# Reordering the input phase of a two-layer diffusion step: inputs first, squares folded on VectorE, seven accumulators, the condition store moved behind the last activation

## The chip, the cores and the metric

The program runs on one core of a Trainium2 chip, as one launch. The metric is the device time of one execution in microseconds. The engines of the core are named as in the profile: PE (TensorE matmul), PEld (its weight loads), DVE (VectorE), ACT (ScalarE), POOL (GpSimd) and SP (SyncE, which here only issues DMAs). A suffix q, as in SPq or ACTq, marks an instruction of an engine's own queue, here always the issue of a DMA.

## The reference

One inference step through two layers over 128 context tokens and 256 latent tokens, 384 in all, of width 2048. Layer 0 mixes RWKV-7 heads and a Fourier mixer, layer 1 is windowed attention. What the change touches is the entry of layer 0:

```python
sh_p, sc_p, g_p = _modulation(c_ctx, mod_w[layer], mod_b[layer])   # silu(cond) @ w + b, split in three
sh_s, sc_s, g_s = _modulation(c, mod_w[layer], mod_b[layer])
hp = _rmsnorm(xp, norm_pre[layer]) * (1.0 + sc_p) + sh_p
hs = _rmsnorm(xs, norm_pre[layer]) * (1.0 + sc_s) + sh_s
...
proj = h @ w_in          # r, k, v, the low-rank inputs, gates and the Fourier inputs
```

So the first projection needs the mean of the squares of each token, and a shift and a scale that come out of a product of the two conditions with a 2048 x 6144 matrix of 4-byte numbers, of which layer 0 needs 2/3 at its entry (32 loads of 1 MB).

## The kernel before

All matrices are held with the channel on the partition (128) and the 384 tokens along the row. A projection is done as three matmuls for each 128x128 block of weights (high and low part of the weights and of the activations: `hhi`, `hlo`, `whi`, `wlo`), 128x384 each.

**The stream of weights.** `Stream` issues 256 KB loads `raw<-we` on SP's queue into two buffers. ACT casts a loaded unit to `whi` (line 260), DVE subtracts to get `wlo` (line 261), and three such pairs may be held. A unit feeds 12 projection matmuls. `plan` puts the units into the order in which the input phase uses them.

**The input phase** is `layer0_in`. It loads the modulation weights in 32 loads `mraw<-modw` of 1 MB into seven buffers, also on SP's queue; `mod_unit` multiplies each with the conditions (`ps_mod<-mraw,silu`). After each four of them ACT copies the sums out (`mrow`, line 331), PE turns them into columns (`ps_mt`), and DVE adds the bias (line 338). Four loads give the shift of a block of four channel tiles, the next four its scale; there are four such blocks, b = 0 to 3. The inputs `xT` come in four loads of 768 KB behind the first four modulation loads. ACT squares each of the 16 channel tiles (`sq`, line 649), and PE adds them up over the partitions with a matrix of ones (`ps_ss`). After the reciprocal root, `make_h` makes the normalised activations of a block: two ACT instructions a tile, then a cast and a subtraction on DVE. Each block of activations is then fed at once to the accumulators that are open: `low` (256 wide, two units a block) and r, k, v of head pair 0 and r of head pair 1, six units a block, 24 in all. A generator list `first` names them, and `pieces` hands out one unit a step:

```python
        ahead = rkv(0, (None, self.pw, self.pw)) + rkv(1, (self.pw, None, None))
        first = [(self.proj_cm(256, acts, low_done), 2)] + [(g, 1) for g in ahead[:4]]
```

`None` means a bank of the PSUM pool `pa` (three banks), `self.pw` one of `pw` (five banks), which `ps_mod` and `ps_mt` use as well.

**What sets the order.** A scheduler orders the instructions of each engine when the program is built, by priority and by its own idea of durations; the queue of each engine then runs in that order. Each DMA of SP and ACT signals one of eight counters, DMAHW0 to DMAHW7, which are given out in turn over both queues. A DMA that takes a counter again waits until the DMA that had it before has landed.

**The condition store.** `build` writes the 2 x 2048 conditions to DRAM (`sd<-cth`, line 604, on ACT's queue), where they are read back much later (`srow<-sd`, line 812). The store is 16 KB in runs of four numbers (16 bytes), 1024 runs.

**After the input phase** the projections go on, interleaved with the RWKV work (`wkv_elem`, `wkv_lower`, `wkv_solve`, `wkv_chain`) and with the remaining modulation columns, whose weights come in 512 KB loads `rawf<-modw` (line 795) into one buffer; each feeds four PE groups `ps_mod<-rawf,silu`, and the next load may be issued when they are done.

Of the kernel before, what the change touches and what calls it, by code (L numbers as in the profile page):

```python
# [11 lines left out]
F32 = mybir.dt.float32  # L12
# [8 lines left out]
KT = 16  # L21
# [284 lines left out]
class K:  # L306
# [69 lines left out]
    def plan(self):  # L376

        A = self.A
        w = [("w", A[n][i]) for n in ("we", "weo", "wo", "woo") for i in range(A[n].shape[0])]
        n0 = A["we"].shape[0]  # L380
        n1 = n0 + A["weo"].shape[0]
        for n in (n1, len(w)):
            w[n - 4:n] = [x + (i,) for i, x in enumerate(w[n - 4:n])]

        w[:24] = [w[i] for b in range(4) for i in (2 * b, 2 * b + 1, 8 + b, 12 + b, 16 + b, 20 + b)]
        out, at = [], 0
        for a, b, jobs in ((n0 - 56, n1 - 10, DVE_MODS[0]), (n1 + 48, len(w) - 68, DVE_MODS[1])):
            m = self.mod_items(jobs)
            if jobs is DVE_MODS[0]:

                q = self.mod_items(PE_MODS)
                m = [x for i in range(12) for x in m[i:i + 1] + q[8 * i // 12:8 * (i + 1) // 12]]
            m = list(chain.from_iterable(m))
            out += w[at:a]
            for i in range(b - a):
                out += m[len(m) * i // (b - a):len(m) * (i + 1) // (b - a)]
                out.append(w[a + i])
            at = b
        return out + w[at:]
# [120 lines left out]
    def make_h(self, pool, kt, src, sc, sh):  # L520
# [4 lines left out]
        for cnd, sl in ((1, slice(0, TP)), (0, slice(TP, T))):  # L525
            nc.scalar.activation(h[:, sl], src[:, sl], AF.Identity, bias=sh[:, m, cnd:cnd + 1],
                                 scale=sc[:, m, cnd:cnd + 1])
        hi = self.hp.tile([128, T], F32R, name="hhi", tag="hhi", bufs=KT)
# [30 lines left out]
    def build(self):  # L559
# [4 lines left out]
        with ExitStack() as ctx:  # L564
# [36 lines left out]
            self.sd = self.dp.tile([4, 2, 128, 4], F32, name="sd")  # L601
            sq = th.rearrange("p (q c k) -> p q c k", q=4, c=2)
            nc.vector.tensor_copy(sq, self.silu[:, 0:32].rearrange("p (q k c) -> p q c k", q=4, c=2))
            nc.scalar.dma_start(self.sd.rearrange("q c p k -> p q c k"), sq)
            self.macc = {}
# [8 lines left out]
    def layer0_in(self, acts, first):  # L614
# [20 lines left out]

        for _ in range(4):
            load()
        xT = ip.tile([128, KT, T], F32, name="xT")
        for b in range(4):
            nc.sync.dma_start(xT[:, 4 * b:4 * b + 4], A["xT"][:, 4 * b:4 * b + 4])  # L640
        for _ in range(3):
            load()
        mod(4)
        ones = ip.tile([128, 128], F32, name="ones")
        nc.vector.memset(ones, 1.0)
        ps = self.pa.tile([128, 512], F32, name="ps_ss", tag="acc")
        for kt in range(KT):
            sq = ip.tile([128, T], F32, name="sq", tag="sq", bufs=2)
            nc.scalar.activation(sq, xT[:, kt], AF.Square)
            self.mm(ps[:, :T], ones, sq, start=(kt == 0), stop=(kt == KT - 1))  # L650
        rs = ip.tile([128, T], F32, name="rs")
# [6 lines left out]
        for b in range(4):  # L658
# [7 lines left out]
            for i in range(7):  # L666
                mod(1)
                if i >= 1:
                    next(pieces[i - 1])
        self.close("mp")  # L670
# [3 lines left out]
    def layer0_mix(self):  # L674
# [20 lines left out]

        ahead = rkv(0, (None, self.pw, self.pw)) + rkv(1, (self.pw, None, None))
        first = [(self.proj_cm(256, acts, low_done), 2)] + [(g, 1) for g in ahead[:4]]
        self.layer0_in(acts, first)
# [24 lines left out]
        def proj_lane():  # L723
# [4 lines left out]
            for j in range(1, 8):  # L728

                gens = ahead[4:] if j == 1 else rkv(j)  # L730
                for g in gens:
# [855 lines left out]
```

## Time and profile before

| what | us |
|---|---|
| median of 3 runs | 1600.47 |
| lowest and highest run | 1600.28 and 1605.43 |
| profiled execution, its own time | 1596.4 |
| its span (first to last instruction) | 1594.6 |

The profiled execution lies 4.1 us below the median of the three runs. The span leaves out 1.8 us that lie around it. Times in the views are counted from the start of the span.

### The profile page before, as it was taken

The numbers are of one execution on the slowest core, as the hardware profiler recorded it, in microseconds if no ns is written. First come the engines' busy times: TensorE is split into PE (matmuls) and PEld (weight loads), VectorE is DVE, ScalarE is ACT, GpSimd is POOL, SyncE is SP. The second block draws the span as 40 slices with busy tenths as digits, with TensorE's granted clock in tenths as the row PEclk, the third lists the DMA queues.
The fourth block names the chain that finished last, engine by engine and source line by source line (L and its number), as shares of the span: only waits on it lengthen the run. The fifth ranks groups of instructions, "written<-read, shape, count | busy, mean of one in ns | idle before, by whom it ended". The sixth has DMA issues, their size and how long they took to land.

```text
span 1594.6 us, 30005 instructions
## 1 busy us (share of the span) xinstructions
PE 1507.3 (95%) x11488; PEld 1275.6 (80%) x11488; DVE 1069.1 (67%) x2584; ACT 810.9 (51%) x1771; POOL 3.9 (0%) x21
## 2 busy tenths in 40 slices
PE   7789999989998999999999998999999999999997
PEld 2557778767776778879998778988888889998777
DVE  1426896687777685574665755899878999653344
ACT  3326756857656655454333335744556555343332
POOL 0000000000000000000000000000000000000000
PEclk9899999999999999999999999899999999999999
DMA  9985352354333243444558664565322444447443
GB/s 365 375 311 164 123 160 78 102 167 122 97 107 110 86 143 90 132 152 126 174 189 325 211 207 144 200 225 204 100 73 73 133 132 140 125 122 242 125 120 139
DMA packets 120246, 255.74 MB, mean 160 GB/s; under 512 B 12324, under 2 KB 45220, under 8 KB 109732
## 3 DMA queue, kind: packets, MB, share of 16 engines
q1 hardware_dynamic: 111528, 235.97, 44.8%
q10 hardware_dynamic: 8576, 17.86, 3.2%
q8 instruction: 90, 1.47, 0.4%
q14 instruction: 52, 0.43, 0.1%
HBM read 246.40 MB, written 7.39 MB: 159 GB/s over the span
## 4 chain that ended last, share of the span: by engine, by line
PE 64%; DVE 16%; DMA 11%; ACT 6%; issue 3%; ACTq 0%; DVEq 0%; SPq 0%
PE acc L404 31%; PE acct L404 16%; DMA rawf<-modw 5%; DVE wlo L261 3%; PE ps_mod L406 3%; DVE junk L350 2%; DMA raw<-we 2%; DMA mraw<-modw 1%; DMA raw<-modw 1%; PE ps_o L410 1%; PE ps_v L410 1%; PE ps_pv L410 1%; ACT whi L260 1%; PE ps_s L410 1%; PE ps_sa L410 1%
## 5 line engine op out<-in xcount | busy, mean ns | idle before, releaser
L260 ACT CAST whi<-raw 128x512 fp32r<-128x512 f32 x480 | 295.5, 621 | 444.7 <-PE acc L404 196.5
L261 DVE TENSOR_TENSOR wlo<-raw,whi 128x512 fp32r<-128x512 f32 x480 | 327.5, 688 | 275.6 <-ACT whi L260 270.8
L404 PE MATMUL acc<-hhi,whi 128*128 128x384 f32 x1376 | 478.3, 348 | 12.5 <-ACT whi L260 5.7
L404 PE MATMUL acc<-hlo,whi 128*128 128x384 f32 x1376 | 472.9, 344 | 0.0
L404 PE MATMUL acc<-hhi,wlo 128*128 128x384 f32 x1376 | 470.7, 343 | 1.7 <-DVE wlo L261 1.3
L404 PEld LDWEIGHTS acc<-hhi,whi 128*128 128x128 f32 x1376 | 261.3, 190 | 44.2 <-issue 18.1
L404 PEld LDWEIGHTS acc<-hlo,whi 128*128 128x128 f32 x1376 | 261.3, 190 | 13.7 <-issue 11.9
L404 PEld LDWEIGHTS acc<-hhi,wlo 128*128 128x128 f32 x1376 | 260.9, 190 | 11.1 <-issue 5.5
L350 DVE SCALAR_TENSOR_TENSOR junk<-raw,srow 128x512 f32<-128x512 f32 x224 | 154.1, 688 | 8.6 <-DMA raw<-modw 5.2
L404 PE MATMUL acct<-whi,yhi 128*128 128x512 f32 (+1 forms) x432 | 154.4, 358 | 2.4 <-DVE yb L1318 2.1
L404 PE MATMUL acct<-wlo,yhi 128*128 128x512 f32 (+1 forms) x432 | 153.9, 356 | 0.0
L404 PE MATMUL acct<-whi,ylo 128*128 128x512 f32 (+1 forms) x432 | 153.7, 356 | 0.0
L404 PEld LDWEIGHTS acct<-whi,yhi 128*128 128x128 f32 x432 | 81.5, 189 | 20.7 <-DVE yb L1318 6.5
L404 PEld LDWEIGHTS acct<-whi,ylo 128*128 128x128 f32 x432 | 81.5, 189 | 12.4 <-issue 0.2
L404 PEld LDWEIGHTS acct<-wlo,yhi 128*128 128x128 f32 x432 | 81.5, 189 | 11.8
L406 PE MATMUL ps_mod<-rawf,silu 128*32 128x256 f32 x112 | 35.0, 395 | 22.5 <-DMA rawf<-modw 22.3
L406 PE MATMUL ps_mod<-mraw,silu 128*32 128x512 f32 x64 | 35.5, 668 | 9.7 <-DMA mraw<-modw 9.7
L1118 DVE TENSOR_TENSOR work<-work 128x30 f32<-128x30 f32 (+14 forms) x120 | 39.2, 327 | 2.1
L1120 DVE TENSOR_TENSOR work<-work 128x30 f32<-128x30 f32 (+14 forms) x120 | 39.2, 327 | 1.9
L1538 DVE TENSOR_REDUCE ast<-ps_sa 128x1 f32<-128x384 f32 x64 | 25.3, 415 | 20.3 <-PE ps_sa L410 20.1
L406 PEld LDWEIGHTS ps_mod<-rawf,silu 128*32 128x32 f32 x112 | 7.7, 108 | 36.2 <-DMA rawf<-modw 25.6
L410 PE MATMUL ps_mod<-rawf,silu 128*32 128x256 f32 x336 | 35.9, 395 | 0.0
(331 smaller groups left out, 2286.5 us busy)
## 6 DMA issues: line engine op xcount, KB each, us to landing
raw<-we SPq DMA_DIRECT2D x200, 256.0 KB, 2.9
raw<-wo SPq DMA_DIRECT2D x160, 256.0 KB, 2.7
raw<-modw SPq DMA_DIRECT2D x36, 1024.0 KB, 5.2
mraw<-modw SPq DMA_DIRECT2D x32, 1024.0 KB, 8.9
rawf<-modw SPq DMA_DIRECT2D x56, 512.0 KB, 3.9
raw<-weo SPq DMA_DIRECT2D x64, 256.0 KB, 2.9
raw<-woo SPq DMA_DIRECT2D x64, 256.0 KB, 2.7
G<-gd ACTq DMA_DIRECT2D x4, 1024.0 KB, 7.4
```

Of the source, the lines that this page charges most:

```text
L260: k.nc.scalar.copy(hi, raw)
L261: k.nc.vector.tensor_tensor(lo, raw, hi, op=ALU.subtract)
L350: nc.vector.scalar_tensor_tensor(junk, raw[:, 512 * i:512 * i + 512], 1.0, self.srow[:, c], op0=ALU.mult, op1=ALU.mult, accum_out=self.dac ...
L404: op(*args, **kw)
L406: self.head.append(op(*args, **kw).ins)
L410: op(*args, **kw)
L1118: TT(tv, X[:, s + 1:32, s:s + 1].to_broadcast([128, n, s]), X[:, s:s + 1, 0:s].to_broadcast([128, n, s]), op=ALU.mult)
L1120: TT(X[:, s + 1:32, 0:s], X[:, s + 1:32, 0:s], tv, op=ALU.add)
L1538: nc.vector.tensor_reduce(st[:, 0, i:i + 1], src[i], axis=AX.X, op=ALU.max)
```

## The change

In `layer0_in` the four loads of the inputs go to the head of SP's queue, behind two units of weights, and the first seven modulation loads follow in one go. The squares are taken by ACT in four instructions of four tiles each; DVE adds the four tiles to one in two instructions; PE does one `ps_ss` matmul for each four tiles, four instead of 16, and the first four modulation units stand behind it instead of ahead of it. Seven accumulators (k of head pair 1 is added, in `pw`) take a unit in each block instead of six, so 28 units belong to the input phase. The condition store is made after the last `make_h`: its ACT issue is tied behind the last activation.

```diff
-        w[:24] = [w[i] for b in range(4) for i in (2 * b, 2 * b + 1, 8 + b, 12 + b, 16 + b, 20 + b)]
+        w[:28] = [w[i] for b in range(4) for i in (2 * b, 2 * b + 1, 8 + b, 12 + b, 16 + b, 20 + b, 24 + b)]
...
-            sq = th.rearrange("p (q c k) -> p q c k", q=4, c=2)
-            nc.vector.tensor_copy(sq, self.silu[:, 0:32].rearrange("p (q k c) -> p q c k", q=4, c=2))
-            nc.scalar.dma_start(self.sd.rearrange("q c p k -> p q c k"), sq)
+            self.th = th
...
-        for _ in range(4):
-            load()
         xT = ip.tile([128, KT, T], F32, name="xT")
         for b in range(4):
             nc.sync.dma_start(xT[:, 4 * b:4 * b + 4], A["xT"][:, 4 * b:4 * b + 4])
-        for _ in range(3):
+        for _ in range(7):
             load()
-        mod(4)
         ones = ip.tile([128, 128], F32, name="ones")
         nc.vector.memset(ones, 1.0)
+
         ps = self.pa.tile([128, 512], F32, name="ps_ss", tag="acc")
-        for kt in range(KT):
-            sq = ip.tile([128, T], F32, name="sq", tag="sq", bufs=2)
-            nc.scalar.activation(sq, xT[:, kt], AF.Square)
-            self.mm(ps[:, :T], ones, sq, start=(kt == 0), stop=(kt == KT - 1))
+        for b in range(4):
+            sq = ip.tile([128, 4, T], F32, name="sq", tag="sq", bufs=2)
+            nc.scalar.activation(sq, xT[:, 4 * b:4 * b + 4], AF.Square)
+            nc.vector.tensor_tensor(sq[:, 0:2], sq[:, 0:2], sq[:, 2:4], op=ALU.add)
+            nc.vector.tensor_tensor(sq[:, 0], sq[:, 0], sq[:, 1], op=ALU.add)
+            self.mm(ps[:, :T], ones, sq[:, 0], start=(b == 0), stop=(b == 3))
+        mod(4)
...
             for i in range(7):
                 mod(1)
-                if i >= 1:
-                    next(pieces[i - 1])
+                next(pieces[i])
+
+        sq = self.th.rearrange("p (q c k) -> p q c k", q=4, c=2)
+        nc.vector.tensor_copy(sq, self.silu[:, 0:32].rearrange("p (q k c) -> p q c k", q=4, c=2))
+        with self.tc.issue_after(self.last_h.ins):
+            nc.scalar.dma_start(self.sd.rearrange("q c p k -> p q c k"), sq)
...
-        ahead = rkv(0, (None, self.pw, self.pw)) + rkv(1, (self.pw, None, None))
-        first = [(self.proj_cm(256, acts, low_done), 2)] + [(g, 1) for g in ahead[:4]]
+        ahead = rkv(0, (None, self.pw, self.pw)) + rkv(1, (self.pw, self.pw, None))
+        first = [(self.proj_cm(256, acts, low_done), 2)] + [(g, 1) for g in ahead[:5]]
...
-                gens = ahead[4:] if j == 1 else rkv(j)
+                gens = ahead[5:] if j == 1 else rkv(j)
```

Where the scheduler then puts things is seen at three places. The first is the head of SP's queue, its first rows (`raw` is a unit of projection weights, `mraw` a modulation load). Before:

```order
L236 DMA raw<-we 128x512 x2
L628 DMA mraw<-modw 128x2048 x4
L640 DMA xT<-xT 128x1536 x4
L628 DMA mraw<-modw 128x2048 x14
L236 DMA raw<-we 128x512 x2
L628 DMA mraw<-modw 128x2048
```

With the change:

```order
L236 DMA raw<-we 128x512 x2
L636 DMA xT<-xT 128x1536 x4
L626 DMA mraw<-modw 128x2048 x17
L236 DMA raw<-we 128x512 x2
L626 DMA mraw<-modw 128x2048
```

The inputs stand ahead of all modulation loads, and 17 of these instead of 18 stand ahead of the third and fourth unit of weights.

The second place is ACT's queue where block b = 2 gets its activations (`h_688` and so on are the four tiles of the block, `sh`, `sc` its shift and scale). Before:

```order
L331 COPY mrow<-ps_mod 128x512
L526 ACTIVATE h_688<-xT,sh_107,sc_108 128x128
L526 ACTIVATE h_688<-xT,sh_107,sc_108 128x256
L526 ACTIVATE h_695<-xT,sh_107,sc_108 128x128
L526 ACTIVATE h_695<-xT,sh_107,sc_108 128x256
L526 ACTIVATE h_702<-xT,sh_107,sc_108 128x128
L526 ACTIVATE h_702<-xT,sh_107,sc_108 128x256
L526 ACTIVATE h_709<-xT,sh_107,sc_108 128x128
L526 ACTIVATE h_709<-xT,sh_107,sc_108 128x256
L260 CAST whi<-raw 128x512 x3
```

With the change:

```order
L526 ACTIVATE h_695<-xT,sh_105,sc_106 128x128
L526 ACTIVATE h_695<-xT,sh_105,sc_106 128x256
L526 ACTIVATE h_702<-xT,sh_105,sc_106 128x128
L526 ACTIVATE h_702<-xT,sh_105,sc_106 128x256
L260 CAST whi<-raw 128x512
L526 ACTIVATE h_709<-xT,sh_105,sc_106 128x128
L526 ACTIVATE h_709<-xT,sh_105,sc_106 128x256
L526 ACTIVATE h_716<-xT,sh_105,sc_106 128x128
L526 ACTIVATE h_716<-xT,sh_105,sc_106 128x256
L260 CAST whi<-raw 128x512 x3
```

One cast of a unit of weights now stands between the second and the third tile of the block instead of behind the fourth.

The third place is SP's queue at the end of the input phase, with the counters that each issue waits for. With the change the store `sd` takes counter DMAHW7 on ACT's queue, right behind the last activation, and SP has these rows (`rawf` is a later modulation load):

```order
L236 DMA raw_850<-we 128x512 [waits DMAHW5_49,DVE_49]
L798 DMA rawf_1084<-modw 128x4x256 [waits PE_49]
L236 DMA raw_880<-we 128x512 [waits DMAHW6_49,DVE_49]
L236 DMA raw_928<-we 128x512 [waits DMAHW7_49,DMAHW0_49,DVE_49]
L798 DMA rawf_1102<-modw 128x4x256 [waits DMAHW2_49,PE_49]
```

Before, the store had counter DMAHW0 and stood near the start, and the sixth modulation load (`mraw_129`) took that counter next:

```order
L640 DMA xT_122<-xT 128x1536 [waits DMAHW6_49]
L628 DMA mraw_127<-modw 128x2048 [waits DMAHW7_49]
L628 DMA mraw_129<-modw 128x2048 [waits DMAHW0_49]
L628 DMA mraw_131<-modw 128x2048 [waits DMAHW1_49]
L628 DMA mraw_138<-modw 128x2048 [waits DMAHW2_49,PE_49]
```

The load that has to wait for the store to land was a modulation load near the start; now it is `raw_928`, a unit of weights (the 26th of 28), with the second `rawf` load queued behind it.

## Rows read from the trace of the kernel before

**Rows 1.** The page: span, and part 1 for PE.
```profile
span 1594.6 us, 30005 instructions
PE 1507.3 (95%) x11488; PEld 1275.6 (80%) x11488; DVE 1069.1 (67%) x2584; ACT 810.9 (51%) x1771; POOL 3.9 (0%) x21
```

**Rows 2.** Windows: busy us of each engine, granted clock, DMA share, GB/s.
```profile
24.00:28.00 4.00, 4.00 (x11) 1.77 (x9) 0.00 (x0) 2.24 (x5) 0.00 (x0) 1.00 0.47 144
28.00:62.00 34.00, 25.68 (x154) 12.28 (x152) 13.25 (x16) 11.38 (x21) 0.00 (x0) 0.90 1.02 421
100.00:124.00 24.00, 23.77 (x137) 16.01 (x138) 4.15 (x9) 4.69 (x8) 0.46 (x4) 0.93 0.67 252
...
200.00:250.00 50.00, 47.08 (x459) 38.97 (x460) 47.69 (x128) 32.06 (x59) 0.13 (x1) 1.00 0.46 143
```

**Rows 3.** Timeline of SP's issues, 11 to 30 us: start, duration.
```profile
11.18 0.43 SPq L628 DMA_DIRECT2D mraw<-modw  x1
25.80 3.03 SPq L628 DMA_DIRECT2D mraw<-modw  x6
```

**Rows 4.** Waits of SP's queue, 0 to 30 us: total, times, longest.
```profile
SPq L628 <- DMA sd<-cth: 14.2, 1, 14.2
```

**Rows 5.** DMA issues, 0 to 30 us: KB each, median us to landing.
```profile
sd<-cth ACTq DMA_DIRECT2D x1, 16.0 KB, 18.6
```

**Rows 6.** Packets of ACT's DMA queue, 11 to 14 us and 25 to 25.2 us.
```profile
q10 hardware_dynamic: 166, 0.00, 3.1%
...
q10 hardware_dynamic: 58, 0.00, 16.3%
```

**Rows 7.** Timeline of PE, 60 to 124 us: start, duration, idle before and releaser.
```profile
63.33 0.69 PE L404 MATMUL acc<-hhi,whi 128*128 128x384 f32 x1 [2.51 <-ACT whi L260]
...
98.99 0.44 PE L404 MATMUL acc<-hhi,whi 128*128 128x384 f32 x1 [3.08 <-ACT whi L260]
...
100.07 0.44 PE L404 MATMUL acc<-hhi,wlo 128*128 128x384 f32 x1 [0.46 <-DVE wlo L261]
...
123.07 0.81 PE L410 MATMUL ps_mt<-sel,mrow 128*128 128x2 f32 x6
```

**Rows 8.** Timeline of DVE and ACT, 94 to 130 us.
```profile
94.10 0.17 DVE L338 TENSOR_TENSOR sc<-ps_mt,modb 128x8 f32<-128x8 f32 x1 [9.16 <-PE ps_mt L410]
...
94.50 1.86 ACT L526 ACTIVATE h<-xT,sh,sc 128x128 f32<-128x128 f32 x4 [1.55 <-DVE sc L517]
...
98.33 1.12 ACT L260 CAST whi<-raw 128x512 fp32r<-128x512 f32 x2
...
129.07 0.35 ACTq L899 DMA_DIRECT2D scan<-cscan  x1
```

**Rows 9.** Groups by line, 0 to 46 us: busy, mean ns, idle before.
```profile
L404 PE MATMUL ps_ss<-sq,ones 128*128 128x384 f32 x32 | 14.6, 607 | 0.0
...
L649 ACT ACTIVATE sq<-xT 128x384 f32<-128x384 f32 x16 | 8.3, 522 | 7.3 <-PE ps_ss L404 6.7
L661 DVE TENSOR_TENSOR xT<-xT,rs 128x1536 f32<-128x1536 f32 x4 | 6.8, 1752 | 0.0
...
L653 DVE RECIPROCAL rs<-rs 128x384 f32<-128x384 f32 x1 | 2.6, 2552 | 15.3 <-ACT rs L652 15.3
```

**Rows 10.** The windows view for the modulation matmuls alone (tile mraw).
```profile
63.30:124.00 60.70, 16.86 (x128) 2.98 (x128) 0.94 0.77 293
```

**Rows 11.** Waits of PE, 120 to 150 us.
```profile
PE ps_mod L406 <- DMA rawf<-modw: 3.1, 2, 1.9
```

**Rows 12.** The chain that ended last, 120 to 150 us: start, duration.
```profile
136.54 4.80 DMA rawf<-modw
...
142.03 4.54 PE acc L404 x25
```

**Rows 13.** The page, part 6: KB each, median us from issue to landing.
```profile
raw<-we SPq DMA_DIRECT2D x200, 256.0 KB, 2.9
```

**Rows 14.** Waits of PE, 130 to 700 us.
```profile
PE ps_mod L406 <- DMA rawf<-modw: 22.3, 20, 4.8
```

More of the change, by code (lines that the diff above doesn't have):

```diff
@@ L525, in make_h @@
         for cnd, sl in ((1, slice(0, TP)), (0, slice(TP, T))):
-            nc.scalar.activation(h[:, sl], src[:, sl], AF.Identity, bias=sh[:, m, cnd:cnd + 1],
-                                 scale=sc[:, m, cnd:cnd + 1])
+            self.last_h = nc.scalar.activation(h[:, sl], src[:, sl], AF.Identity, bias=sh[:, m, cnd:cnd + 1],
+                                               scale=sc[:, m, cnd:cnd + 1])
         hi = self.hp.tile([128, T], F32R, name="hhi", tag="hhi", bufs=KT)
```

## The prediction

> **What bounds the kernel now.** The page comes first: PE is busy for 1507 of 1594.6 us [rows 1], so the stages after the entry are short of PE time, and what can be won lies where PE stands idle, which the page puts into its first slices. The windows view then splits the entry. From 28 to 62 us the DMA engines move 421 GB/s with a share of 1.02 [rows 2]: the modulation loads set the pace there, and PE waits. From 24 to 28 us the share is only 0.47 [rows 2], in the middle of a stage that waits for loads. SP's timeline says why: a modulation load is issued at 11.18, the next one at 25.80 [rows 3], and the waits of SP's queue name the condition store as releaser, 14.2 us [rows 4]. The store took 18.6 us to land [rows 5], although it is 16 KB: from 11 to 14 us, beside the large loads, ACT's queue got 166 packets through, which is 166 / 16 engines in 3 us, or 0.29 us each; from 25 to 25.2 us, with the large packets gone, it got 58 through, or 0.055 us each [rows 6].
>
> The second thing that bounds the entry is PE itself, from 63.33 on: there it waited 2.51 us for the third unit of weights [rows 7], which stands behind 18 modulation loads, and then it works nearly without a gap, but for one at 96 to 100 us. There the scale of block 2 was written at 94.10, ACT made eight activations from 94.50, and only at 98.33 came to the casts of weights that PE needed [rows 8]; PE stood for 3.08 us, and 0.46 more for `wlo` [rows 7].
>
> **The change, part by part.** The sum is made on the profiled execution, 1596.4 us, and carried to the median, 1600.47, by subtraction.
>
> *Squares.* ACT takes four tiles in one instruction; that costs at most 4 x 0.522 = 2.1 us [rows 9]. The DVE adds are 768 and 384 wide, each less than the 1.75 us of the 1536-wide product [rows 9]. PE has four `ps_ss` matmuls, 8 rows of 0.61 instead of 32 (14.6 us) [rows 9]. The four inputs are 3.1 MB, 7.5 us at 421 GB/s, and are in at about 13 us. Behind the last of them stand at most 2.1 + 3.5 + 1.2 + 2 (root and its table) + 2.6 (reciprocal) + 7.0 (products), which is 31.4. The scale of block 0 needs eight modulation loads behind the inputs: 13 + 8 x 2.5 = 33. So all of it is hidden, and I put it at 0; if it were late by some us, only the 24 matmuls on the two units loaded at the start would move, and these end well before 58 us. The 11 us of PE time saved by fewer `ps_ss` is worth nothing for the same reason: loads set the pace there.
>
> *a. The wait for the store* leaves the start. The DMA engines then don't run dry: 4 us x (1 - 0.47) = 2.1 us [rows 2].
>
> *b. One modulation load fewer* stands ahead of the third unit: 1.049 MB at 421 GB/s is 2.5 us. The Trainium skill (DMA: Bandwidth & Descriptors, section Bandwidth) says that loads from HBM are bound by about 358 GB/s a core; by that this term would be an estimated 2.9 us and the sum 0.4 us more. The row shows 421 over 34 us, and the row decides. With a and b PE gets its third unit at 63.33 - 4.6 = 58.7.
>
> *c. The gap at block 2.* One cast now stands behind four activations instead of eight: 94.50 + 1.86 = 96.4 instead of 98.33 [rows 8], 1.9 us. One modulation unit of PE, 16.86 / 16 = 1.05 us [rows 10], moves out of the gap and has to be done elsewhere. Net 0.9.
>
> *d. The clock.* From 100 to 124 us, behind the gap, the granted clock was 0.93 [rows 2], which cost 24 x 0.07 = 1.7 us. A shorter gap may keep it. Between 0 and 1.7 I take half, 0.8.
>
> *e. PSUM.* Four of the five `pw` banks are now held by accumulators, so a modulation group can't start before DVE has read the columns of the group before it. Where a modulation unit stands right behind `ps_mt` on PE (two places), that costs the DVE instruction, 0.17 us [rows 8], and the handovers, together 0.3 each: -0.6. Elsewhere projections stand between. Bounds: 0, and twice as much.
>
> a to e give 5.7 us. The four units of k that move into the phase change nothing in this: they are 48 matmuls of 4.54 / 25 = 0.18 us [rows 12] that PE has to do in any case.
>
> *f. The end of the phase.* The last `ps_mt` ended at 123.07 + 0.81 = 123.88 [rows 7]; now 24 more projection matmuls stand ahead of it (4.4 us), so it ends at 123.88 - 5.7 + 4.4 = 122.6. The last activation comes 5.2 us later (`scan` was issued right behind it at 129.07, [rows 8]); there the store is issued: 127.8. When does it land? 64 packets for each engine at 0.055 us are 3.5 us; the fixed part I take from a 256 KB load, 2.9 us less the 0.6 of its bytes at 421 GB/s [rows 13], 2.3. That is 5.8, if nothing else moves. The loads of weights beside it are some 16 packets of 2 KB and 32 of 1 KB an engine, 2.5 us at 26 GB/s an engine: 8.3. The other end is the 18.6 of [rows 5], beside 8 KB packets. The row for free packets is nearer; I take 7.0, the middle of 5.8 and 8.3.
>
> Until then SP stands at `raw_928`, and behind it the second `rawf` load. So that is issued at 127.8 + 7.0 + 0.4 = 135.2 and lands 4.8 us later [rows 12], at 140.0. PE comes to it after 79 matmuls and one group: 122.6 + 14.4 + 0.5 = 137.5, and waits 2.5 us. Without the store it would wait for its buffer only, to 138.6. Before, the two such waits there were 3.1 us [rows 11]; the first now vanishes, since its load stands ahead of fewer units. So f is +0.6, with 1.8 at a store of 5.8 us and -0.7 at 8.3.
>
> Sum: 2.1 + 2.5 + 0.9 + 0.8 - 0.6 + 0.6 = 6.3 us. That gives 1590.1 for an execution like the profiled one, and 1594.2 against the median. What a measurement here can tell from no change is about 0.3%, 4.8 us, so this is not far beyond it.
>
> **The rivals.**
>
> *The store blocks SP (slower).* If beside the weight loads it takes the 18.6 us of before, SP is free at 146.4, the `rawf` load lands at 151.6, PE waits 14.1 us instead of 3.1, and a to f become -5.3: 1605.8. It breaks even where the landing takes 13.3 us. For it speaks that the only landing on record is 18.6; against it that the packets beside it then were four to eight times as large. Chance 0.12.
>
> *The gain is absorbed.* In the RWKV stage DVE is busy 47.69 of 50 us (200 to 250) [rows 2]. Its first chain starts with k of head pair 0, which comes behind the second `rawf` wait and so no earlier than before. If DVE and that chain set the pace, PE only gains slack, and the time stays at 1599 to 1602. Against it: PE is 95% busy [rows 1], and head pair 1, which the first solve needs as well, has its k 48 matmuls earlier. Chance 0.28. With it goes a PSUM wait of more than a microsecond at each of the six modulation groups (e at ten times its price): 1600, chance 0.03.
>
> *More than that.* PE waits 22.3 us for `rawf` loads at 20 places between 130 and 700 us [rows 14]. The new order shifts all of them; if a third goes, 7 us more are won: 1587. Chance 0.13. A shift that loses as much is in the case above.
>
> **How the numbers follow.** My forecast has 0.44, of which 0.02 ends within 0.3%. Faster by over 0.3%: 0.42 + 0.13 = 0.55. Within: 0.28 + 0.03 + 0.02 = 0.33. Slower: 0.12. The predicted time is 1594.2. The range goes from 1586 (the third rival, a little further) to 1602 (the end of the second); what is left out is most of the first rival and the tails. The likeliest case alone, with c to f at their bounds, is 1591 to 1597.
>
> **What would show it.** After the change SP's waits near the start no longer name `sd`, and the windows from 24 to 28 us have a DMA share near 1 (a). The first `acc` matmul that waits for a cast comes near 58.7 (a, b). At block 2 PE waits less than 2 us for `whi` (c), and the granted clock behind it is nearer 1 (d). PE's waits name DVE `sh` or `sc` for under 1 us in all (e). SP waits for `sd` near 130 us, by 1 to 4 us, and PE's second `rawf` group waits 1 to 4 us (f). The prediction is wrong if that wait is over 10 us, or if the entry ends 6 us earlier by PE's count of matmuls and the lead is gone at 300 us.

## The result and the profile after

The change made the kernel slower: 1608.09 us (median of 14 runs, 1604.53 to 1620.46) against 1601.48 us for the kernel before (14 runs, 1596.69 to 1607.46) on the same chip. The ratio is 1.0052, with a 95% interval of 1.0034 to 1.0070. A second measurement on another chip (run e7_after_again below) gave 1607.36 against 1602.55 and 1.0034 (1.0014 to 1.0053). The forecast was 1594.2 us, a gain.

The profiled execution of the changed kernel took 1616.38 us, above its median; that of before, 1596.4, was below its own. So no difference of these two traces alone is taken for an effect. Each kernel was profiled once more, in e7_after_again (1604.38 us) and e8_before_again (1604.36 us).

The page of the changed kernel, its span and its engines, beside [rows 1]:

```profile
span 1614.5 us, 29927 instructions
PE 1519.3 (94%) x11464; PEld 1284.9 (80%) x11464; DVE 1076.0 (67%) x2592; ACT 808.2 (50%) x1759; POOL 3.9 (0%) x21
```

PE is busy for 12 us more, though 24 matmuls went. A busy PE at the lower clock takes longer: the result lists a mean granted clock of 0.972 for this execution and 0.984 for that of before.

**The input phase went as forecast.** Windows of the changed kernel, as [rows 2], and the timeline of SP's issues, as [rows 3]:

```profile
24.00:28.00 4.00, 2.53 (x24) 1.13 (x16) 4.00 (x4) 0.59 (x1) 0.00 (x0) 1.00 1.02 422
28.00:62.00 34.00, 25.38 (x139) 13.68 (x140) 6.81 (x15) 7.24 (x14) 0.00 (x0) 0.77 0.97 394
100.00:124.00 24.00, 23.84 (x149) 15.88 (x142) 3.75 (x9) 4.59 (x8) 0.74 (x4) 0.98 0.68 258
```

```profile
1.66 3.56 SPq L636 DMA_DIRECT2D xT<-xT  x4
5.26 39.97 SPq L626 DMA_DIRECT2D mraw<-modw  x17
45.28 0.90 SPq L236 DMA_DIRECT2D raw<-we  x2
```

The DMA share between 24 and 28 us rose from 0.47 to 1.02. Seventeen loads now follow the inputs without a hole. The granted clock from 28 to 62 us is 0.77 instead of 0.90, but in the second traces of both kernels it is 0.85, so this is not taken for an effect. Timeline of PE in the changed kernel, as [rows 7]: the first `acc` matmul that waits for a cast, the one behind the scale of block 2, and the last `ps_mt`:

```profile
58.25 0.69 PE L404 MATMUL acc<-hhi,whi 128*128 128x384 f32 x1 [2.76 <-ACT whi L260]
...
94.69 0.69 PE L404 MATMUL acc<-hhi,whi 128*128 128x384 f32 x1 [1.54 <-ACT whi L260]
...
122.82 0.81 PE L410 MATMUL ps_mt<-sel,mrow 128*128 128x2 f32 x6
```

The third unit of weights comes at 58.25 instead of 63.33; the gap at block 2 is 1.54 us instead of 3.08 and 0.46. The waits of PE for columns, 56 to 124 us, and for `rawf` loads, 120 to 150 us (as [rows 11]), and the store's landing (as [rows 5]):

```profile
PE ps_mod L406 <- DVE sc L338: 0.3, 1, 0.3
PE ps_mod L406 <- DVE sh L338: 0.3, 1, 0.3
```

```profile
PE ps_mod L406 <- DMA rawf<-modw: 0.2, 1, 0.2
```

```profile
sd<-cth ACTq DMA_DIRECT2D x1, 16.0 KB, 3.5
```

**The lead is gone at the first solve.** Counted along ACT's timeline, the 29th cast of weights stands at 152.69 in the kernel before and at 146.72 in the changed one. That is a lead of 6.0 us. Fifty us later it is a lag. Timeline of DVE and ACT, first solve (`work<-DB`) and start of the first chain (`work<-v`); first the kernel before in its second trace, then the changed kernel:

```profile
197.54 1.91 DVE L1112 STREAM_TRANSPOSE work<-DB 128x1024 f32<-128x1024 f32 x1 [0.71 <-ACT DB L1063]
249.21 1.10 ACT L1175 COPY work<-v 128x256 f32<-128x256 f32 x4
```

```profile
203.06 1.95 DVE L1115 STREAM_TRANSPOSE work<-DB 128x1024 f32<-128x1024 f32 x1
255.49 1.12 ACT L1178 COPY work<-v 128x256 f32<-128x256 f32 x4
```

The second trace of the changed kernel has 201.16 and 253.57, the first of before 198.24 and 249.28. So the first solve comes 3 to 6 us later, and the first chain 4 to 6.

The chain itself makes this up: the second solve starts at the same time again. Timeline of DVE, the kernel before in its second trace, then the changed kernel (the other two traces have 326.27 and 324.67):

```profile
326.20 2.00 DVE L1112 STREAM_TRANSPOSE work<-DB 128x1024 f32<-128x1024 f32 x1
```

```profile
326.48 1.96 DVE L1115 STREAM_TRANSPOSE work<-DB 128x1024 f32<-128x1024 f32 x1
```

What is missing by then is projection work on PE, which is counted below, under theory F.

Why the first solve is late is seen in ACT's queue. Timeline of ACT, the kernel before in its second trace (`kk`, `sq`, `p`, `tha` belong to head pair 0, `work` to pair 1):

```profile
145.54 0.61 ACT L955 ACTIVATE kk<-k,par 128x384 f32<-128x384 f32 x1
...
149.87 0.53 ACT L961 ACTIVATE sq<-sq 128x384 f32<-128x384 f32 x1
...
155.19 0.57 ACT L910 ACTIVATE k<-acc,imu 128x384 f32<-128x384 f32 x1
...
156.24 1.36 ACT L977 ACTIVATE p<-ps_lo,wa 128x256 f32<-128x256 f32 x4 [0.22 <-PE ps_lo L404]
...
157.98 0.87 ACT L980 ACTIVATE p<-p 128x768 f32<-128x768 f32 x1
```

And the changed kernel:

```profile
147.25 0.61 ACT L958 ACTIVATE kk<-k,par 128x384 f32<-128x384 f32 x1
...
152.32 0.62 ACT L958 ACTIVATE work<-k,par 128x384 f32<-128x384 f32 x1 [1.08 <-DVE k L916]
152.96 1.28 ACT L964 ACT_TABLE_LOAD   x1
154.25 0.53 ACT L964 ACTIVATE sq<-sq 128x384 f32<-128x384 f32 x1
...
158.98 0.58 ACT L913 ACTIVATE v<-acc,imu 128x384 f32<-128x384 f32 x1 [0.56 <-PE acc L404]
159.82 0.48 ACT L980 ACTIVATE p<-ps_lo,wa 128x256 f32<-128x256 f32 x1 [0.26 <-PE ps_lo L404]
...
162.22 1.28 ACT L964 ACT_TABLE_LOAD   x1
...
167.61 0.86 ACT L983 ACTIVATE p<-p 128x768 f32<-128x768 f32 x1
```

With k of pair 1 at hand, its `kk` stands ahead of pair 0's logarithm and waits for DVE; the copy of its v stands ahead of pair 0's tanh and waits for PE; its own logarithm costs two changes of table in the middle of pair 0's work. `p<-p`, on which pair 0's scans on DVE wait, comes at 167.61 instead of 157.98. The windows from 145 to 175 us show what DVE loses (third pair of numbers), 23.33 us busy before (second trace) and 19.59 after:

```profile
145.00:175.00 30.00, 29.00 (x174) 22.99 (x173) 23.33 (x59) 24.47 (x47) 0.13 (x1) 1.00 0.47 155
```

```profile
145.00:175.00 30.00, 29.55 (x173) 24.03 (x172) 19.59 (x50) 25.09 (x49) 0.00 (x0) 1.00 0.45 138
```

### The profile page after: what moved, and what is told of

Its sections match the earlier page's. It is cut to its first block, busy times and chain, and to the rows that moved or that the text cites. A ratio compares the mean times of both kernels' runs of the same rounds, so it can differ in the third digit from the quotient of the medians.

```text
span 1614.5 us, 29927 instructions
## 1 busy us (share of the span) xinstructions
PE 1519.3 (94%) x11464; PEld 1284.9 (80%) x11464; DVE 1076.0 (67%) x2592; ACT 808.2 (50%) x1759; POOL 3.9 (0%) x21
## 4 chain that ended last, share of the span: by engine, by line
PE 63%; DVE 17%; DMA 11%; ACT 6%; issue 3%; SPq 0%; DVEq 0%; ACTq 0%
PE acc L404 29%; PE acct L404 15%; DMA rawf<-modw 4%; DVE wlo L261 4%; PE ps_mod L406 3%; DMA raw<-we 3%; DVE junk L350 2%; DMA raw<-modw 2%; PE ps_v L410 1%; PE ps_o L410 1%; ACT whi L260 1%; PE ps_pv L410 1%; PE ps_s L410 1%; DMA mraw<-modw 1%; PE ps_lo L404 1%
## 5 line engine op out<-in xcount | busy, mean ns | idle before, releaser
L260 ACT CAST whi<-raw 128x512 fp32r<-128x512 f32 x480 | 295.8, 622 | 454.2 <-PE acc L404 195.6
L406 PE MATMUL ps_mod<-rawf,silu 128*32 128x256 f32 x112 | 35.1, 395 | 20.3 <-DMA rawf<-modw 19.8
L331 ACT COPY mrow<-ps_mod 128x256 f32<-128x256 f32 (+1 forms) x24 | 11.0, 460 | 58.0 <-PE ps_mod L410 58.0
```

The costliest lines, as they stand in the source:

```text
L260: k.nc.scalar.copy(hi, raw)
L331: nc.scalar.copy(rows, acc[:, :n])
L406: self.head.append(op(*args, **kw).ins)
```

## The experiments

Theory A: the seventh accumulator does this harm. Rivals: B, the clock; C, the store at its new place; later ones are named where they came up. All times are medians in us; "first solve" and "first chain" are the starts of the rows above (`work<-DB` and `work<-v`), in each run's trace. The medians of the kernel before beside these runs lie from 1602.1 to 1603.2. The ratio is not that of the two medians, so the last two columns can differ a little, as for e4.

| run | first solve | first chain | median | ratio to before (95%) |
|---|---|---|---|---|
| e1_six | 195.6 | 246.4 | 1603.54 | 1.0012 (0.9992 to 1.0033) |
| e2_only_seven | 206.0 | 257.3 | 1606.86 | 1.0029 (1.0012 to 1.0047) |
| e3_only_store | 196.4 | 247.1 | 1599.36 | 0.9979 (0.9958 to 1.0000) |
| e4_only_inputs | 198.4 | 249.1 | 1603.59 | 1.0023 (1.0003 to 1.0043) |
| e5_hold | 203.0 | 259.5 | 1613.24 | 1.0077 (1.0049 to 1.0105) |
| e6_store_seven_hold | 205.3 | 261.8 | 1616.45 | 1.0098 (1.0067 to 1.0129) |
| e7_after_again | 201.2 | 253.6 | 1607.36 | 1.0034 (1.0014 to 1.0053) |
| e8_before_again | 197.5 | 249.2 | 1603.02 | 1.0000 (0.9976 to 1.0025) |
| e9_pair0_first | 200.2 | 252.8 | 1606.14 | 1.0025 (1.0010 to 1.0039) |
| e10_store_pair0_first | 200.0 | 252.4 | 1605.13 | 1.0022 (1.0004 to 1.0040) |
| e11_v_seventh | 207.1 | 260.7 | 1612.31 | 1.0056 (1.0034 to 1.0078) |
| e12_seven_store | 208.3 | 259.8 | 1605.60 | 1.0022 (1.0004 to 1.0039) |
| e13_five_store | 212.2 | 269.3 | 1616.91 | 1.0089 (1.0063 to 1.0115) |
| e14_store_again | 193.9 | 246.0 | 1597.25 | 0.9959 (0.9940 to 0.9977) |
| e15_five | 211.8 | 267.9 | 1613.14 | 1.0073 (1.0047 to 1.0100) |
| e16_store_pair1_first | 200.7 | 253.5 | 1602.26 | 0.9994 (0.9975 to 1.0014) |
| e17_pair1_first | 204.1 | 258.3 | 1610.98 | 1.0069 (1.0044 to 1.0093) |
| e18_store_both_first | 199.6 | 251.9 | 1603.52 | 1.0015 (0.9993 to 1.0036) |

### The parts alone

**e1_six.** The changed kernel with the lines of the seventh accumulator as they were:

```diff
-        ahead = rkv(0, (None, self.pw, self.pw)) + rkv(1, (self.pw, self.pw, None))
+        ahead = rkv(0, (None, self.pw, self.pw)) + rkv(1, (self.pw, None, None))
```

> The change with six accumulators instead of seven; inputs first, squares on VectorE and the late store stay. Theory A (the seventh accumulator does the harm: k of head pair 1 comes 14 us earlier, its element-wise work runs into that of pair 0 on ACT and DVE, and the first solve comes 5 us later): the entry still ends some 4 us earlier, the kk of pair 1 is back near 165 us, and the time is 1594 to 1598, 0.2 to 0.5% below before. Theory B (any new order draws other half-speed stretches of TensorE's clock, and these make the time): still 1604 or more, with half-speed stretches that add up to well over the 52 us of before. Theory C (the store behind the last activation holds SP at the end of the phase): still 1604 or more, with SP late there.

The first solve is back at 195.6 and the kk of pair 1 at 163.6, as A said; the time, 1603.54, is about 4 us below the changed kernel (1608.09 and 1607.36, on other chips) and not below before. A accounts for part of the loss.

**e2_only_seven.** The kernel before with

```diff
-        ahead = rkv(0, (None, self.pw, self.pw)) + rkv(1, (self.pw, None, None))
+        ahead = rkv(0, (None, self.pw, self.pw)) + rkv(1, (self.pw, self.pw, None))
```

and the lines on `w` and `pieces` that go with it.

> The kernel before with the seventh accumulator alone. Theory A: 1604 to 1610, 0.3 to 0.6% above before, with the kk of pair 1 near 155 us, elements of pairs 0 and 1 interleaved, and the first solve some 5 us later than 198. Theory B: slower only as its half-speed stretches add up to more than 52 us. Theory C: no slower than before, about 1599, since the store stands where it stood and the gap at block 2 is 1 to 2 us shorter.

Slower by 0.3%, first solve at 206.0, kk of pair 1 at 154.8: for A, against C.

**e3_only_store.** The kernel before, with the store's three lines behind the last `make_h` and tied to `last_h`, as in the change.

> The kernel before with the store alone moved behind the last activation. Theory A: SP's 14.2 us wait at the start is gone, the third unit of weights comes 2 us earlier, and the time is 1598 to 1601, no slower than before. Theory B: anything from 1597 to 1610, going with the sum of half-speed stretches. Theory C: 1604 or more.

SP no longer waits for `sd`. The store lands in 4.7 us:

```profile
sd<-cth ACTq DMA_DIRECT2D x1, 16.0 KB, 4.7
```

Faster by 0.2%, with 1.0000 as the end of the interval (e14 repeats it): C falls. On the same chip e1, which differs from e3 by the inputs and the squares alone, takes 4.2 us more (1603.54 against 1599.36), although its first chain starts no later. So the inputs part costs time by itself, and not through the first chain.

**e4_only_inputs.** The changed kernel with six accumulators and the store back in `build`.

> The kernel before with the inputs loaded first and the squares added on VectorE, with six accumulators and the store at the start. Theory A: loads set the pace at the entry, so 11 us less PE work for the sum of squares is worth little there: 1598 to 1602. Theory B: anything from 1597 to 1610, going with the sum of half-speed stretches. Theory C: 1598 to 1602 too.

The entry is no faster, as A and the forecast had it. The four runs price a and b one by one. Timeline of PE, the first `acc` matmul that waits for a cast, in e2, e3 and e4 (one fence for each):

```profile
60.92 0.44 PE L404 MATMUL acc<-hhi,whi 128*128 128x384 f32 x1 [2.75 <-ACT whi L260]
```

```profile
60.66 0.44 PE L404 MATMUL acc<-hhi,whi 128*128 128x384 f32 x1 [2.57 <-ACT whi L260]
```

```profile
63.44 0.69 PE L404 MATMUL acc<-hhi,whi 128*128 128x384 f32 x1 [5.28 <-ACT whi L260]
```

Against 63.33 [rows 7] the seventh accumulator brings 2.4 us there (b), the store 2.7 (a), the inputs alone nothing; the changed kernel has 5.1. (Store and seven without the inputs, e12 below, have it at 60.82: the two add up only with the inputs at the head.) The 0.2% that e4 lost by the ratio (0.6 us by the median) do not show in the order of its trace: at the 29th, 61st and 131st cast of weights (152, 292 and 654 us) it is within 0.3 us of the first one of before. They go with the granted clock, whose mean over all runs is 0.977 for e4 and 0.980 for before on that chip.

**e7_after_again** and **e8_before_again** are the two kernels unchanged.

> The changed kernel itself, beside the others on one chip. Theory A: 1605 to 1611, and in its trace, whatever its clock, the first solve again 5 us later than before's 198. Theory B: the loss against before goes with the half-speed stretches of the RWKV stage, so that a run with as few of them as before ends near before's time.

> The kernel before itself, for a second trace. Its first profiled execution was 5 us below the median of its runs. If that is the clock alone, the stages up to 600 us agree within 1 us with the first trace, and the further half-speed stretches lie near 640 to 1070 us, where the other kernels have them.

The loss and the late first solve are there again (2.9 to 3.6 us later). The two traces of before agree at the first chain (249.3 and 249.2) and at the second solve (326.3 and 326.2); then the granted clock of the second falls. Windows of the first trace of before, then of the second, 320 to 380 us:

```profile
320.00:350.00 30.00, 27.00 (x241) 22.77 (x237) 25.51 (x66) 16.95 (x31) 0.00 (x0) 1.00 0.57 180
350.00:380.00 30.00, 27.44 (x340) 21.07 (x341) 28.33 (x74) 19.68 (x40) 0.12 (x1) 1.00 0.53 160
```

```profile
320.00:350.00 30.00, 27.89 (x238) 24.25 (x233) 24.27 (x62) 16.05 (x30) 0.00 (x0) 0.94 0.54 173
350.00:380.00 30.00, 26.54 (x227) 19.23 (x225) 24.88 (x65) 15.11 (x31) 0.10 (x1) 0.83 0.44 136
```

The level of 1.2 GHz held for about 14 us (2 x 30 x 0.06 and 2 x 30 x 0.17), and the second pair of chains starts at 384.6 instead of 378.9. So the expectation that they agree up to 600 us was wrong: the same program gets its half-speed stretches at different places, and two traces of it differ by 8 us (spans 1594.6 and 1602.6).

### Which wait in ACT's queue

**e5_hold** lets pair 1's work out only when pair 0 has made `EC`; **e6_store_seven_hold** does this without the new inputs and squares.

```diff
+                if j == 1:
+                    yield "half_elem0"
                 yield from self.wkv_elem(j, sts[j])
...
+        if j == 0:
+            yield "set", "half_elem0"
```

> The changed kernel, but the element-wise work of head pair 1 may only be given out once pair 0 has made its decays (EC). Theory A (the harm is that the two pairs interleave): pair 0's scans on DVE come back from 169 us towards 160, the first solve from 203 towards 195, and the time is 1596 to 1602, 0.4% or more below the changed kernel on the same chip. Theory D (what holds pair 0 up is not pair 1's element-wise work but the copy of pair 1's v out of PSUM, which ACT's queue puts ahead of pair 0's tanh): the scans stay at 166 or later, the first solve at 200 or later, and the time within 0.2% of the changed kernel. Theory B (clock alone): time goes with the half-speed stretches whatever the first solve does.

> The kernel before with the store moved, seven accumulators and the hold of e5_hold; inputs and squares as before. Theory A: 1595 to 1599, at or below the kernel with the store alone (1599.4), with the first solve near 196. Theory D and theory B: 1602 to 1608, about that of seven accumulators alone less the 2 to 3 us of the store.

Both are worse than without the hold. Pair 0's scans come at 165.3, only 2 to 3 us earlier, while pair 1's go from 175 to 176 us to 182.0 and 184.3. D's first solve (200 or later) came true, its time did not. Theory A in its simple form, that interleaving alone is the harm, falls.

**e9_pair0_first** gives pair 0's work a lane of its own with 100 more priority in the changed kernel; **e10_store_pair0_first** does it on e3.

```diff
-LEAD = (0, 0, 300, 300, 0, 0, 0, 0, 100)
+LEAD = (0, 0, 300, 300, 0, 100, 0, 0, 0, 100)
...
                 if j == 2:
+                    yield "elem0"
                     yield "elem1"
...
-elem_lane((0, 2, 3, 4, 5, 6, 7)), elem_lane((1,))
+elem_lane((0,)), elem_lane((2, 3, 4, 5, 6, 7)), elem_lane((1,))
```

> The changed kernel, with the element-wise work of head pair 0 in a lane of its own, 100 ahead in the scheduler's priority, so that ACT's queue has pair 0's logarithm and tanh ahead of pair 1's kk and of the copy of pair 1's v. Theory A2 (the seventh accumulator makes k of pair 1 ready early, its work and the copy of v get ahead of pair 0's in ACT's queue, DVE stands idle between 145 and 175 us and is short of that time up to the first solve): pair 0's scans start by 161, the first solve by 199, and the time is 1598 to 1603, below the changed kernel's 1605 to 1608. Theory E (pair 0's place doesn't matter, the first solve waits for pair 1, and the seven accumulators cost through something else): the first solve stays at 201 or later, and the time at 1605 or more.

> The kernel before with the store moved, six accumulators, and pair 0's element-wise work 100 ahead in priority. Theory A2: the chain of pair 0 sets the pace of the RWKV stage, so the first solve comes earlier than 196 and the time falls below the 1599.4 of the store alone, to 1594 to 1598. Theory E: as the store alone, 1598 to 1601, with the first solve at 196.

In e9 the scans start at 157.1, before those of the kernel before, yet the first solve stays at 200.2: A2 falls too. e10 says why. Timeline of DVE in e10, the last products of pair 0 (`kk,E`) and pair 1 (`work,SC`), and the first solve:

```profile
165.68 0.29 DVE L1037 SCALAR_TENSOR_TENSOR AR<-kk,E 128x128 f32<-128x128 f32 x1
...
193.37 1.16 DVE L1037 SCALAR_TENSOR_TENSOR AR<-work,SC 128x256 f32<-128x256 f32 x4
...
200.01 1.92 DVE L1115 STREAM_TRANSPOSE work<-DB 128x1024 f32<-128x1024 f32 x1 [0.72 <-ACT DB L1066]
```

The same in e3:

```profile
172.72 0.28 DVE L1036 SCALAR_TENSOR_TENSOR AR<-kk,E 128x128 f32<-128x128 f32 x1
...
189.70 1.15 DVE L1036 SCALAR_TENSOR_TENSOR AR<-work,SC 128x256 f32<-128x256 f32 x4
...
196.41 1.91 DVE L1114 STREAM_TRANSPOSE work<-DB 128x1024 f32<-128x1024 f32 x1 [0.72 <-ACT DB L1065]
```

Pair 0 is 7 us earlier, pair 1 3.7 us later, the first solve 3.6 us later, and the median is 6 to 8 us above the store alone. The solve takes both pairs, so here the later one decides, and what brings the first one forward at its cost is a loss. (The new lanes also move the input phase of e10: its first `acc` matmul that waits for a cast is at 63.28, in e3 at 60.66.)

### How many accumulators, and which

**e11_v_seventh** takes v of pair 1 as the seventh in place of k; **e12_seven_store** is the changed kernel without its inputs part.

```diff
-        ahead = rkv(0, (None, self.pw, self.pw)) + rkv(1, (self.pw, self.pw, None))
+        ahead = rkv(0, (None, self.pw, self.pw)) + rkv(1, (self.pw, None, self.pw))
+        ahead[4], ahead[5] = ahead[5], ahead[4]
```

> The changed kernel with v of pair 1 as the seventh accumulator instead of k. The entry is the same (as many units, as many banks of PSUM), but k of pair 1 comes as late as before. Theory A2: the entry's lead of 6 us lasts, pair 0's scans come by 161, the first solve by 198, and the time is 1597 to 1603. Theory E (seven accumulators cost by their number, by PSUM or by the units of weights that they move, whichever they are): 1605 or more.

> The kernel before with the store moved and seven accumulators, inputs and squares as before. If the parts add up (store -3, seven +4): 1602 to 1606, the first solve at 204. If it takes all three parts for the loss of the changed kernel: 1598 to 1601.

In e11 pair 1's kk comes late again (163.2), but the first solve is later still, 207.1, and so is the time. It isn't k as such. e12's time, 1605.60, is what the parts add up to, at the upper end; its first solve, 208.3, is 4 us later than that.

**e13_five_store** and **e15_five** go the other way, on e3 and on the changed kernel.

```diff
-            ... rkv(1, (self.pw, None, None))
-        first = ... for g in ahead[:4]]
+            ... rkv(1, (None, None, None))
+        first = ... for g in ahead[:3]]
```

**e14_store_again** is e3 once more.

> The kernel before with the store moved and five accumulators instead of six (r of head pair 1 goes back behind the input phase). Theory F (what an accumulator more does in the phase is taken from the projections that fill TensorE while the first chain of pairs 0 and 1 runs, 250 to 326 us; that stage is paced by the chain, so the lead is lost there): with five, the entry ends some 4 us later, projections in 250 to 326 us take 35 us or more of PE instead of 31, and the time is 1596 to 1601, no more than with six. Theory G (time won at the entry is kept, and seven lose for another reason): 1602 to 1606, 4 us above the store alone.

> The kernel with the store alone moved, once more, beside the others. If its gain of 0.2% is real: 1597 to 1600. If it was the draw of the half-speed stretches: 1601 to 1604.

> The changed kernel with five accumulators. Theory F: at or below the 1603.5 of six (1599 to 1604), and below the changed kernel. Theory G: 1606 or more, as the entry ends later than with six.

Theory F (the lead is taken from the projections that fill PE while the first chains run) came from the windows view for the tile `acc` alone, PE (busy time and matmuls, granted clock, DMA share, GB/s), kernel before (second trace) and changed kernel:

```profile
0.00:150.00 150.00, 65.58 (x310) 0.94 0.82 313
150.00:250.00 100.00, 60.56 (x316) 0.98 0.43 137
250.00:326.00 76.00, 31.21 (x144) 1.00 0.32 103
```

```profile
0.00:150.00 150.00, 72.50 (x345) 0.92 0.83 315
150.00:250.00 100.00, 60.16 (x308) 1.00 0.48 147
250.00:326.00 76.00, 19.42 (x81) 0.96 0.30 90
```

Twelve us of projection work are missing while the first chains run, and the granted clock is lower there. Counted from the start, the changed kernel is 35 projection matmuls ahead at 150 us (345 against 310), 27 ahead at 250, and 36 behind at 326 (734 against 770). The other two traces give 348 against 308 at 150 us and again 734 against 770 at 326.

But with five accumulators the 76 us hold 26.03 us (e13), not 35, and five are slower than six, in e13 also than seven (e12): F falls, and so does G as it stood, since 10 to 18 us (e15 over e1, e13 over e3) are far more than the 4 us that it allowed. What F counted holds in another form: by 326 us all nine traces with six accumulators have 768 to 780 projection matmuls done, the nine with seven 732 to 746, the two with five 745 and 746. The ratios of the six lie from 0.9959 to 1.0023, those of the others from 1.0022 to 1.0098. Why six give more is not tested. In e13 pair 1's r comes behind the phase, its tanh starts at 184.64, DVE is busy for 15.34 of the 25 us from 175 to 200 (22.51 in before's second trace), and the first solve comes at 212.2. Windows of e13:

```profile
175.00:200.00 25.00, 25.00 (x155) 21.29 (x155) 15.34 (x35) 18.85 (x36) 0.00 (x0) 1.00 0.37 114
```

e14 confirms that the store alone is a gain: 0.9959, with 1 outside of the interval.

### Does the time follow the first chain?

**e16_store_pair1_first** and **e18_store_both_first** give 100 more priority on e3 to pair 1's lane, and to both; **e17_pair1_first** to pair 1's on the changed kernel. In e9's line the three lanes get 0, 0, 100 (e16, e17) and 100, 0, 100 (e18) instead of 100, 0, 0.

> The store moved, six accumulators, and the element-wise work of head pair 1 (not pair 0) 100 ahead in priority. Theory H (the first chain can start only when the first solve has the work of both pairs, so pair 1's, the later one, sets the pace; over the kernels so far the median is 1603 plus 0.7 for each us by which the first chain starts after 249 us): pair 1's last product comes before the 190 us of the store alone, the first chain starts by 245, and the time is 1595 to 1599. If pair 0's work loses as much as pair 1's wins: first chain at 247 or later, 1599 to 1604. Theory G (the end of the input phase sets the time): as the store alone, 1597 to 1600, whatever the first chain does.

> The changed kernel with the element-wise work of head pair 1 100 ahead in priority. Theory H: the time follows the start of the first chain: at 249 or earlier 1599 to 1605, at 255 or later 1605 to 1611. Theory G: 1605 to 1608 as the changed kernel, since the input phase is the same.

> The store moved, six accumulators, and the element-wise work of both pairs 100 ahead in priority. With pair 0 alone ahead, pair 1's last product came 4 us later and the time was 1605. Theory H: it depends on pair 1: if its last product comes at 190 us or before, 1595 to 1600, if at 193 or later, 1602 to 1607. Theory G: 1597 to 1600 in either case.

G falls: the changed kernel, e5, e9, e11 and e17 have one and the same input phase, with the first `acc` matmul that waits for a cast at 58.21 to 58.31 in all five, and take from 1606 to 1613 us. (On e3 the new lanes move that matmul from 60.66 to 62.09 in e16 and 61.90 in e18, so these two are no clean comparison.) In e16 and e18 pair 1's last product does come early (187.5 and 188.8), and the first solve late all the same (200.7, 199.6), so "the later pair decides" is not the whole rule either. H missed in e18, where pair 1's last product came before 190 us and 1595 to 1600 was forecast. Its relation holds only roughly: by 1603 plus 0.7 for each us after 249, e16, e17 and e18 should take 1606.2, 1609.5 and 1605.0, and took 1602.3, 1611.0 and 1603.5. Over the changed kernel and the 18 runs the first chain's start and the ratio have a correlation of 0.84, with 0.75 us for each us; single kernels lie up to 5.6 us off the line. No kernel whose first chain starts after 250 us is measurably faster than before, and both runs that are faster (e3, e14) start it at 247.1 or earlier. But e1 starts it at 246.4 and is not faster. A correlation over kernels does not show that the late start causes the loss, and the second solve, level again at 326 us, speaks against a delay that is simply handed on.

## Why the prediction was wrong

*a and b* were right in size: 2.1 and 2.5 us forecast, 2.7 and 2.4 measured one by one, and together 58.25 for 58.7. But they add up only beside the inputs part: without it the third unit comes at 60.82 (e12). So the squares, put at 0, are worth 2.6 us at this place. Why is not tested.

*c* was right in its cause and nearly in its size: the gap is 2.0 us shorter, 1.9 forecast. Whether 0.9 of it is left in the end no run tells.

*d* was right where it was put: from 100 to 124 us the granted clock is 0.98 and 1.00 in the two traces, 0.93 in both of before, and 24 us x 0.05 to 0.07 is 1.2 to 1.7 us, 0.8 forecast. What it left out is the clock ahead of the gap: from 58 to 100 us it is 0.87 and 0.88 instead of 0.96 in both of before, and 42 us x 0.08 to 0.09 is an estimated 3.4 to 3.8 us lost. The last `ps_mt` ends at 122.82 + 0.81 = 123.63, in the second trace at 122.65, for a forecast of 122.6.

*e* was right: two waits of 0.3 us.

*f* was better than forecast: the store landed in 3.5 us instead of 7.0, SP did not wait for it, and PE's waits for `rawf` from 120 to 150 us are 0.2 us instead of 3.1 [rows 11]. The first rival, the store that blocks SP, did not occur, and e3 and e14 show that moving it is the one part that pays. The third rival did not occur either: between 130 and 700 us PE waits 19.8 and 14.8 us for `rawf` loads, before 22.3 and 18.1.

So the sum for the input phase held (forecast 6.3, measured 6.0 and 6.3 at the 29th cast in the two pairs of traces). Part of that is luck: f gave 2.3 us more than forecast, and the clock ahead of the gap took some 3.5.

**The step that failed** is the one from there to the end: "PE is 95% busy", so a lead of PE at 124 us was taken off the whole time. The runs showed that the lead does not last: 35 to 40 projection matmuls ahead at 150 us, PE is 36 behind at 326, and 36 x 0.18 us are an estimated 6.5 us of PE. That is the sign of being wrong that the prediction itself gave, a lead gone at 300 us. The rival that the gain is absorbed named the right stage, and the argument that was held against it was the mistake: head pair 1 "has its k 48 matmuls earlier". This did not help the first solve. It put pair 1's work and the copy of its v into ACT's queue among pair 0's, DVE was busy for some 4 us less between 145 and 175 us, and the first chain started 4 to 6 us later, at an input phase that was 6 us shorter. That the seventh accumulator delays the first solve and costs time is shown by e2 against before, and that the order of this work moves the time at an unchanged input phase by e5, e9, e11 and e17. What rule sets the first solve in each order is not settled: neither one pair's wait in ACT's queue (e5, e9) nor the later pair's last product (e16, e18) is the whole of it. How the loss of this stage reaches the end isn't shown either: later on the two traces of the changed kernel lie on both sides of those of before (131st cast at 671.4 and 647.6, before 653.9 and 657.7).

**A second term was wrong**, the inputs and squares at 0. Beside the moved store they cost 4.2 us (e1 against e3). So the parts are: the store gains 0.2 to 0.4% (e3, e14), the seventh accumulator costs 0.3% (e2), the inputs part 0.2 to 0.3% (e4, e1 against e3). Together that is 0.1 to 0.4% lost, where the whole change lost 0.34 and 0.52%.

**What the clock does.** The mean granted clock over all runs was 0.976 and 0.977 for the changed kernel, 0.978 to 0.980 for the kernel before. Over 130 executions of the kernel before beside the experiments, 0.001 less goes with 1.0 us more. At an equal mean clock of 0.977 to 0.979, 58 executions of before average 1603.8 us and 12 of the changed kernel 1607.1. So theory B holds a share, an estimated 2 to 3 us, but 3.3 us are left without it. Of the kernels with six accumulators those with the inputs first have 0.977 (e1, e4), those without 0.978 to 0.982 (before, e3, e10, e14, e16, e18); at 0.977 to 0.979 the 15 executions of e1 and e4 average 1602.9, no more than before. So what the inputs part costs goes with the clock, what the seventh accumulator costs does not. Whether the lower clock is a cause of its own, by PE's smaller load at the entry, or follows from PE's waits, stays open, and no run here tells it.

## What to carry to other kernels

A lead at the end of one stage counts only as far as it reaches what paces the next one. Find the first instruction of the pacing chain (here the first solve) in the trace, list what it needs last, and ask when that is ready, whatever the busy share of PE says. Then count the matmuls of the bound engine at the end of the next stage too: here the chain caught up and the projections beside it did not. When work is moved ahead of such a chain, compare the order on the engines that feed it: an operand that is ready earlier lets its consumers slip in front of the chain's own work in an engine's queue.

## What the runs showed of the hardware that was not expected

The landing of one and the same 16 KB store (runs of 16 bytes) took 18.6 and 18.7 us beside the 1 MB loads at the start, and 3.3 to 5.1 us behind the input phase, over all the traces that have it there, where the forecast allowed 5.8 to 8.3. Two executions of the kernel before, within 0.1 us of each other at the first chain and the second solve, differed by 8 us of span; their mean granted clocks were 0.984 and 0.978.
